# Feed-forward: the weight sums of every second unit made beside the input projection

## The chip, the cores and the metric

The kernel runs on one core of one Trainium2 chip. Its time is the device time of one execution in microseconds (us), of that core. Several executions are timed and the median is given; one execution more is recorded by the hardware profiler. The core has engines that each work through a queue of their own in a fixed order: PE (TensorE, matrix products), DVE (VectorE), ACT (ScalarE), POOL (GpSimd), and SP (SyncE), which in this kernel issues nearly all transfers (DMA) between the memory of the chip (DRAM) and the on-chip memory (SBUF).

## The reference

One layer of a hybrid trunk over 2048 tokens and 16 learned meta tokens, width 1024, all in float32:

```
p = rms_norm(h) @ w_in                      # input projection, 1024 x 3080
oa, ob, oc = rg_lru(p), forgetting_attention(p), rwkv7(p)
h = h + rms_norm(concat(oa, ob, oc) @ w_out)
f = causal_dwconv(rms_norm(h) @ ffn_up)     # 1024 x 5632, then 3 taps in time
gate, val = split(f)
h = h + rms_norm((gelu(gate) * val) @ ffn_down)
```

`rms_norm` divides a row by its root mean square and multiplies by a gain. The change concerns the weights `ffn_up` of the feed-forward part. They are inputs of the kernel and depend on nothing that is computed.

## The kernel before

**Stages.** The input projection runs in three parts of tokens (`for part in range(3)` in `hybrid_block_kernel`, L1978), each with 24 blocks of 128 output columns. Beside parts 1 and 2, and for some time behind them, the recurrences (RG-LRU and RWKV-7) of tokens that are already projected are worked off, a step or two at a time (class `Beside`). Then come attention, the output projection, the up projection of the feed-forward part (`ffn_up`, L1670) and the down projection (class `Down`).

**Precision.** Each operand of a matmul is kept as a high and a low part (`split`, L1574: ACT writes the high part, DVE or POOL the difference), and each product is three matmuls (`mm3`, L168 to L170).

**The up projection** works in three passes (`sup` 0, 1, 2) over blocks of tokens. In each pass it goes over 22 units `j`; a unit is a block of 128 gate columns and the 128 value columns that belong to it. A unit is computed by seven products in the manner of Strassen and Winograd instead of eight: three of them take quarters of the weights as they are (`g0`, `g1`, `v1`) and four take sums of the quarters `g0`, `v0`, `v1`, `g1` (`SUMS`, L1588):

```
s1 = v0 + v1,  s2 = s1 - g0,  s3 = g0 - v0,  s4 = g1 - s2
```

The products stand in `PRODUCTS` (L1524). The same sums serve all three passes. In pass 0 a unit is its "own" (`UpWeights`, L1615): the four raw quarters are loaded (256 KB each, L1634), POOL makes the four sums (L1648), and each sum is stored to DRAM (`scr["us"]`, L1649) as soon as it is made. In passes 1 and 2 all seven weights are loaded, the sums from `scr["us"]`. The weights of unit `j + 1` are prepared during the products of unit `j`. Of the seven low parts of a unit, POOL makes one in pass 0 (product 6) and two in passes 1 and 2 (products 3 and 6), by `POOLED`, L1659; DVE makes the others. Ten buffers (`uq`) hold raw weights and sums.

**Around it.** POOL also multiplies gate and value (`ending`, L1693) and makes sums of the token operands of the next pass (`ffn_sums`, L1570). DVE adds up products in PSUM (L1728, L1731, L1734), does two taps of the convolution (L1687), the low parts (L1576), and normalises the tokens of the next pass: `between` (L2069) calls `ffn_norm` (L1531) in even units, which loads 128 rows `xt` (L1536) and scales them on DVE (L1537).

**Sums of the down weights.** `weight_sums` (L1591) makes sums of the down projection's weights in the same way, ten units of one load of 1 MB, four POOL operations and one store of 1 MB, through a single buffer of four quarters (pool `us`). They are called for between the turns of the input projection (L2012: two of three turns of parts 1 and 2). A turn is one step of the generator `w_in_part` (25 in each of these parts: the gate columns, 22 column blocks, and the last two by token blocks).

**What sets the order.** The program is written in one order, but a planner with a model of the engines (`schedule_with_timeline_sim`, L2165) sets the order of each engine's queue: an instruction may be moved ahead of others when its inputs and its buffer are ready by the model. `tc.issue_after(x)` keeps instructions of the same engine behind `x`. On the chip each queue runs in that fixed order, and an instruction that waits holds those behind it.

**The projection's stores.** `w_in_step` (L203) computes a block of columns for a block of tokens, and SP stores it (L220, L221, L227). Columns of the values (`kind == "v"`) are transposed first and stored a step later (L241, L246).

Of the kernel before, what the change touches and what calls it, by code (L numbers as in the profile page):

```python
# [1 line left out]

# [6 lines left out]
F32 = mybir.dt.float32  # L9
# [4 lines left out]
ALU = mybir.AluOpType  # L14
# [4 lines left out]
P = 128  # L19
# [6 lines left out]
PAD = 64  # L26
A_ROWS = 512
C_ROWS = 1024
FF = 2816
NFF = FF // P  # L30
# [173 lines left out]
def w_in_step(core, pools, psum, weights, block, kind, c0, scr):  # L204

    nc = core.nc
    wh, wl = weights
    st = pools["st"]
    t0, n, tl, hi, lo = block
    ps = psum.tile([P, 512], F32, tag="mm", name=core.n("psp"))  # L210
    for k in range(KD):
        mm3(nc, ps[:, :n], wh[:, k], wl[:, k], hi[:, k], lo[:, k], k == 0, k == KD - 1)
    if kind in ("q", "k"):
        sc = 0.125 if kind == "q" else 1.0
        r0 = c0 - (512 if kind == "q" else 1024)
        oh = st.tile([P, 400], F32R, tag="sth", name=core.n("sth"))
        ol = st.tile([P, 400], F32R, tag="stl", name=core.n("stl"), bufs=1)
        nc.scalar.activation(oh[:, :n], ps[:, :n], AF.Copy, scale=sc)
        nc.vector.scalar_tensor_tensor(ol[:, :n], ps[:, :n], sc, oh[:, :n], op0=ALU.mult, op1=ALU.subtract)
        nc.sync.dma_start(scr[kind + "h"][r0 : r0 + P, t0 : t0 + n], oh[:, :n].bitcast(F32))  # L220
        nc.sync.dma_start(scr[kind + "l"][r0 : r0 + P, t0 : t0 + n], ol[:, :n].bitcast(F32))  # L221
        return
    o = st.tile([P, 400], F32, tag="sth", name=core.n("stp"))
    core.evac(o[:, :n], ps[:, :n])
    if kind != "v":
        r0 = c0 if kind == "a" else c0 - 2056 + A_ROWS
        nc.sync.dma_start(scr["p"][r0 : r0 + P, PAD + t0 : PAD + t0 + n], o[:, :n])  # L227
        return

    def turn():  # L230

        r0 = c0 - 1536
        pt = psum.tile([P, 4, P], F32, tag="mm", name=core.n("psv"))
        for i, (s, rows) in enumerate(tl):
            nc.tensor.transpose(pt[:rows, i], o[:, s - t0 : s - t0 + rows], core.ident[:])
        ot = st.tile([P, 4, P], F32, tag="stv", name=core.n("stv"), bufs=1)
        i0 = 0
        if tl[0][1] < P:
            s, rows = tl[0]
            core.evac(ot[:rows, 0], pt[:rows, 0])  # L240
            nc.sync.dma_start(scr["v"][s : s + rows, r0 : r0 + P], ot[:rows, 0])  # L241
            i0 = 1
        m = len(tl)
        core.evac(ot[:, i0:m], pt[:, i0:m])
        s = tl[i0][0]
        nc.sync.dma_start(  # L246
            scr["v"][s : s + P * (m - i0), r0 : r0 + P].rearrange("(j p) c -> p j c", p=P), ot[:, i0:m]
        )

    return turn  # L250
# [1334 lines left out]

SUMS = ("s2", "s4", "s3", "s1")  # L1588


def weight_sums(core, pool, w_down, scr):  # L1591

    nc = core.nc
    sub = lambda o, x, y: nc.gpsimd.tensor_tensor(o, x, y, op=ALU.subtract)
    for k in range(DOWN_PAIRS):
        t = pool.tile([P, 4, 512], F32, tag="us", name=core.n("ds"))
        nc.sync.dma_start(
            t[:].rearrange("p (i h) c -> p i (h c)", h=2),
            w_down[2 * P * k : 2 * P * (k + 1), :].rearrange("(i p) c -> p i c", p=P),
        )  # L1600
        l0, r0, l1, r1 = (t[:, i] for i in range(4))
        sub(l0, r0, l0)
        sub(r0, r1, r0)
        sub(r1, r1, l0)
        sub(l1, l1, r1)
        nc.sync.dma_start(scr["ds"][k], t[:].rearrange("p s c -> p (s c)"))
        yield
# [7 lines left out]
class UpWeights:  # L1615
# [2 lines left out]

    def __init__(self, core, raws, ring, w_up, scr, j, sup):
        self.core, self.raws, self.ring, self.w_up, self.scr, self.j = core, raws, ring, w_up, scr, j  # L1620
        self.own = sup == 0
        self.raw = {s: self.load(s) for s in ("g0", "v0", "v1", "g1")} if self.own else {}

    def new(self):
# [313 lines left out]
def hybrid_block_kernel(ctx: ExitStack, tc: tile.TileContext, args, out):  # L1938
    a = {s: v[0] if s != "meta_tokens" else v for s, v in args.items()}
    nc = tc.nc  # L1940
    core = Core(tc, ctx)
    scr = scratch(tc, ctx, core)
# [8 lines left out]
    def pool(es, name, bufs, **kw):  # L1951
        return es.enter_context(tc.tile_pool(name=name, bufs=bufs, **kw))
# [11 lines left out]
    with ExitStack() as p1:  # L1964
# [7 lines left out]
        with ExitStack() as p1a:  # L1972
            ps_mm = pool(p1a, "ps_mm", 5, space=PSUM)
            g_pre = spread(pool(p1a, "gpre", 1), a["norm_mix_pre"], "g_pre")
            pools = {"xn": pool(p1a, "xn", 1), "nt": pool(p1a, "nt", 4), "w": pool(p1a, "w", 2), "st": pool(p1a, "st", 2)}
            sums = weight_sums(core, pool(p1a, "us", 1), a["ffn_down"], scr)
            following = w_in_norm(core, pools, ps_mm, x, meta, g_pre, 0)
            for part in range(3):  # L1978
                blocks = following
# [28 lines left out]
                for i, _ in enumerate(units, READY + 1 if part == 0 else 1):  # L2008
                    if i == READY + 1:
                        beside.add(recurrences(core, R, lk, a["fox_f_bias"], scr, blocks, part))  # L2010
                    beside.advance()
                    if part and i % 3:  # L2012
                        next(sums, None)
                run(sums) if part == 2 else None
                if part < 2:
# [12 lines left out]
    with ExitStack() as p3:  # L2028
# [38 lines left out]
        sums, ws, down = [iter(())], [], []  # L2067
# [101 lines left out]
```

## Time and profile before

| | us |
|---|---|
| median of 3 runs | 3058.98 |
| lowest and highest of them | 3055.77, 3062.25 |
| the execution that was profiled, its time | 3059.87 |
| its span, from the first to the last instruction | 3058.1 |
| input projection parts 1 and 2 | about 330 to 845 |
| up projection, passes 0, 1 and 2 | from 1675, 2000 and 2295 to 2590 |

Times in the profile are microseconds from the start of the span. Rows of groups give line, engine, operation, tiles written and read, shapes and count, then after the bar the busy time, the mean of one in nanoseconds, and after the next bar the engine's idle time in front of them and what ended it. Rows of waits read "engine line waited for: total us, times, longest". Rows of the order of time give start, duration and the instruction, with the idle time in front of it in square brackets. PEclk is the share of the full TensorE clock that was granted. "SPq" is SP issuing a transfer; a transfer lands some time later.

### The profile page before, as it was taken

The page shows a single profiled execution, that of the slowest core. Times are in us where ns is not written, and L with a number is a line of the kernel's source. Part 1 is how long each engine was busy: PE and PEld are TensorE (multiplying, and loading weights), DVE is VectorE, ACT ScalarE, POOL GpSimd, SP SyncE. Part 2 cuts the span into 40 slices and gives each one's busy share as a digit, 9 for nine tenths or more (in the row PEclk, how much of TensorE's full clock was granted, in tenths as well). Part 3 has the DMA queues.
Part 4 walks back from the last instruction along what each step waited for, and adds up shares of the span by engine and source line. Part 5 has one row for each costly group of instructions (what it writes and reads, how often), then busy time and mean ns, then how long its engine had stood idle before and what let it go on. Part 6 is the DMA issues. An engine that isn't in the chain of part 4 may idle for free.

```text
span 3058.1 us, 52158 instructions
## 1 busy us (share of the span) xinstructions
PE 2876.4 (94%) x18488; PEld 2468.6 (81%) x18488; DVE 2162.6 (71%) x4232; ACT 1467.4 (48%) x2772; POOL 1312.2 (43%) x1436
## 2 busy tenths in 40 slices
PE   6998999999978999999988999999999999999998
PEld 6987998999855555664567999999999998787876
DVE  6247656676778888677556879887778787547766
ACT  4145344354545445445544545566566665324333
POOL 3310101001134557456723667833453334557765
PEclk8999999999968989999999999999999999999999
DMA  6664333353352346344264555565556565435444
GB/s 213 226 203 143 106 91 112 109 153 114 90 127 73 92 106 166 101 116 107 56 200 138 172 173 170 180 178 170 163 163 171 165 190 172 165 102 171 147 163 145
DMA packets 455477, 443.70 MB, mean 145 GB/s; under 512 B 81472, under 2 KB 372490, under 8 KB 452384
## 3 DMA queue, kind: packets, MB, share of 16 engines
q1 hardware_dynamic: 454832, 439.98, 48.6%
q8 instruction: 145, 2.38, 0.3%
q14 instruction: 116, 0.95, 0.1%
q0 software_dynamic: 384, 0.39, 0.0%
HBM read 314.39 MB, written 125.87 MB: 144 GB/s over the span
## 4 chain that ended last, share of the span: by engine, by line
PE 39%; DVE 7%; DMA 6%; POOL 5%; issue 3%; ACT 2%; SPq 0%; POOLq 0%; DVEq 0%; ACTq 0%
PE psu L168 8%; PE psu L169 7%; PE psu L170 7%; PE psd L170 2%; PE po L682 2%; PE psd L169 2%; PE psd L168 2%; DMA u<-scr_ff 2%; PE pswo L168 2%; PE pswo L170 2%; PE pswo L169 1%; PE mx L530 1%; DMA uq<-in_ffn_up_dram 1%; DVE uw L1576 1%; PE sc L659 1%
## 5 line engine op out<-in xcount | busy, mean ns | idle before, releaser
L168 PE MATMUL psu<-xo,uw 128*128 128x344 f32 x1848 | 592.5, 325 | 27.0 <-ACT xo L1575 7.7
L169 PE MATMUL psu<-xo,uw 128*128 128x344 f32 x1848 | 595.3, 322 | 0.0
L170 PE MATMUL psu<-xo,uw 128*128 128x344 f32 x1848 | 584.9, 321 | 0.0
L168 PE MATMUL psp<-xh,wh 128*128 128x384 f32 (+2 forms) x1152 | 381.0, 331 | 0.0
L170 PE MATMUL psp<-xh,wl 128*128 128x384 f32 (+2 forms) x1152 | 379.0, 329 | 0.0
L169 PE MATMUL psp<-xl,wh 128*128 128x384 f32 (+2 forms) x1152 | 377.5, 328 | 0.0
L168 PEld LDWEIGHTS psu<-xo,uw 128*128 128x128 f32 x1848 | 349.2, 190 | 31.3 <-ACT u L1726 8.2
L1576 DVE TENSOR_TENSOR uw<-uq,uw 128x512 fp32r<-128x512 f32 x352 | 331.4, 948 | 53.1 <-ACT uw L1575 50.9
L169 PEld LDWEIGHTS psu<-xo,uw 128*128 128x128 f32 x1848 | 350.4, 190 | 0.0
L170 PEld LDWEIGHTS psu<-xo,uw 128*128 128x128 f32 x1848 | 348.8, 190 | 0.0
L1575 ACT ACTIVATE uw<-uq 128x512 fp32r<-128x512 f32 x462 | 287.1, 627 | 93.0 <-PE psu L170 48.0
L664 ACT ACTIVATE p<-sc,bias 128x512 f32<-128x512 f32 (+4 forms) x352 | 197.2, 590 | 200.0 <-PE sc L660 165.3
L1687 DVE SCALAR_TENSOR_TENSOR uy<-psu,ffn_cols,uy 128x342 f32<-128x342 f32 (+1 forms) x396 | 223.7, 566 | 71.5 <-ACT uy L1685 70.3
L703 POOL TENSOR_TENSOR acc<-acc,p 128x512 f32<-128x512 f32 (+3 forms) x208 | 229.8, 1107 | 78.4 <-DVE acc L703 32.1
L1693 POOL TENSOR_TENSOR uy<-uy,uy 128x342 f32<-128x342 f32 (+1 forms) x132 | 146.7, 1111 | 218.8 <-DVE uy L1687 99.2
L1576 POOL TENSOR_TENSOR uw<-uq,uw 128x512 fp32r<-128x512 f32 x110 | 158.7, 1443 | 179.2 <-ACT uw L1575 149.9
L170 PEld LDWEIGHTS psp<-xh,wl 128*128 128x128 f32 x1152 | 220.3, 191 | 6.9 <-issue 5.6
L169 PEld LDWEIGHTS psp<-xl,wh 128*128 128x128 f32 x1152 | 220.2, 191 | 6.8 <-issue 5.4
L168 PEld LDWEIGHTS psp<-xh,wh 128*128 128x128 f32 x1152 | 220.3, 191 | 4.2 <-issue 1.9
L533 DVE TENSOR_REDUCE mc<-mx 128x1 f32<-128x400 f32 (+6 forms) x320 | 171.9, 554 | 49.2 <-PE mx L530 46.7
L1576 DVE TENSOR_TENSOR fo<-u,fo 128x896 fp32r<-128x896 f32 x88 | 108.5, 1233 | 122.0 <-ACT fo L1575 122.0
L1648 POOL TENSOR_TENSOR uq<-uq,uq 128x512 f32<-128x512 f32 x88 | 132.1, 1504 | 114.4 <-DMA uq<-in_ffn_up_dram 90.4
(460 smaller groups left out, 6393.3 us busy)
## 6 DMA issues: line engine op xcount, KB each, us to landing
uq<-in_ffn_up_dram SPq DMA_DIRECT2D x220, 256.0 KB
uq<-scr_us SPq DMA_DIRECT2D x176, 256.0 KB
raw<-in_w_in_dram SPq DMA_DIRECT2D x72, 512.0 KB
scr_us<-uq SPq DMA_DIRECT2D x88, 256.0 KB
u<-scr_ff SPq DMA_DIRECT2D x88, 256.0 KB
scr_ff<-uy SPq DMA_DIRECT2D x110, 171.0 KB
q<-scr_qh SPq DMA_DIRECT2D x96, 128.0 KB
ds<-in_ffn_down_dram SPq DMA_DIRECT2D x10, 1024.0 KB
```

What stands on the lines that cost most here:

```text
L168: nc.tensor.matmul(out, ah, bh, start=first, stop=False, skip_group_check=more)
L169: nc.tensor.matmul(out, ah, bl, start=False, stop=False, skip_group_check=more)
L170: nc.tensor.matmul(out, al, bh, start=False, stop=last, skip_group_check=more)
L533: self.reduced = nc.vector.tensor_reduce(mc[:rows, i, ci : ci + 1], ps[:rows, :full], axis=AX.X, op=ALU.max)
L664: last = nc.scalar.activation(p[:rows, :w], ps[:rows, :w], AF.Exp, bias=bias[:rows, j : j + 1])
L682: mm = nc.tensor.matmul(po[at : at + 64, c0:n], v1[:rows, j], p[:rows, : n - c0], start=start and i < 2, stop=end and i + 2 >= len(group), ...
L703: eng.tensor_tensor(a, ps_[0][0][:rows, c0:n] if start and i == 1 else a, p[:rows, : n - c0], op=ALU.add)
L1575: core.nc.scalar.activation(hi, src, AF.Copy)
L1576: (eng or core.nc.vector).tensor_tensor(lo, src, hi, op=ALU.subtract)
L1648: core.nc.gpsimd.tensor_tensor(raw[:], self.raw[x][:], self.raw[y][:], op=op)
L1687: stt(y[:, :n], src[:, i : n + i], cw[:, 44 * i + cc : 44 * i + cc + 1], y[:, :n], op0=ALU.mult, op1=ALU.add)
L1693: core.pooled = nc.gpsimd.tensor_tensor(v[:, :n], g[:, :n], v[:, :n], op=ALU.mult)
```

## The change

The sums of the even units `j` = 0, 2, ... 20 are no longer made in pass 0. A new generator `up_sums` makes them beside the input projection, called behind `weight_sums` in one chain and through the same single buffer: four loads of 256 KB, four POOL operations in place, and two turns later one store of 1 MB; after one turn more the next unit. Its loads and stores are kept behind the store that the input projection issued last in program order (`core.stored`, not renewed by the `v` columns). `SUMS` is reordered so that the four sums stand in `scr["us"]` as they stand in the buffer. The chain is called in every turn of parts 1 and 2, no longer in two of three. In pass 0 odd units stay their own; even ones load all seven weights, as in passes 1 and 2, and by `POOLED` give POOL two low parts.

```diff
-        nc.sync.dma_start(scr[kind + "l"][r0 : r0 + P, t0 : t0 + n], ol[:, :n].bitcast(F32))
+        core.stored = nc.sync.dma_start(scr[kind + "l"][r0 : r0 + P, t0 : t0 + n], ol[:, :n].bitcast(F32))
...
-        nc.sync.dma_start(scr["p"][r0 : r0 + P, PAD + t0 : PAD + t0 + n], o[:, :n])
+        core.stored = nc.sync.dma_start(scr["p"][r0 : r0 + P, PAD + t0 : PAD + t0 + n], o[:, :n])
...
-SUMS = ("s2", "s4", "s3", "s1")
+SUMS = ("s2", "s3", "s1", "s4")
+
+
+def up_sums(core, pool, w_up, scr, after):
+
+    nc = core.nc
+    tt = nc.gpsimd.tensor_tensor
+    for j in range(0, NFF, 2):
+        t = pool.tile([P, 4, 512], F32, tag="us", name=core.n("us"))
+        g0, v0, v1, g1 = (t[:, i] for i in range(4))
+        with after():
+            for o, r0, c0 in ((g0, 0, 0), (v0, 0, FF), (v1, 512, FF), (g1, 512, 0)):
+                nc.sync.dma_start(
+                    o.rearrange("p (k c) -> p k c", c=P),
+                    w_up[r0 : r0 + 512, c0 + P * j : c0 + P * j + P].rearrange("(k p) c -> p k c", p=P),
+                )
+        tt(v1, v0, v1, op=ALU.add)
+        tt(v0, g0, v0, op=ALU.subtract)
+        tt(g0, v1, g0, op=ALU.subtract)
+        tt(g1, g1, g0, op=ALU.subtract)
+        yield
+        yield
+        with after():
+            nc.sync.dma_start(scr["us"][j], t[:].rearrange("p s c -> p (s c)"))
+        yield
...
-        self.own = sup == 0
+        self.own = sup == 0 and j % 2 == 1
...
-            sums = weight_sums(core, pool(p1a, "us", 1), a["ffn_down"], scr)
+            kept = pool(p1a, "us", 1)
+            sums = chain(
+                weight_sums(core, kept, a["ffn_down"], scr),
+                up_sums(core, kept, a["ffn_up"], scr, lambda: tc.issue_after(core.stored.ins)),
+            )
...
-                    if part and i % 3:
+                    if part:
                         next(sums, None)
```

More of the change, by code (lines that the diff above doesn't have):

```diff
@@ L1 @@
+from itertools import chain
 from contextlib import ExitStack, nullcontext
```

## The prediction

> **What bounds the kernel now.** I read the page's summary first, then the busy time of each engine by stage, because the busy share of the span averages stages with different limits. The columns of the stage view are: stretch, its length, then busy time and instruction count of PE, PEld, DVE, ACT and POOL, granted clock, DMA share, GB/s.
>
> ```profile
> span 3058.1 us, 52158 instructions
> ...
> PE 2876.4 (94%) x18488; PEld 2468.6 (81%) x18488; DVE 2162.6 (71%) x4232; ACT 1467.4 (48%) x2772; POOL 1312.2 (43%) x1436
> ```
>
> ```profile
> 46.00:200.00 154.00, 146.81 (x804) 145.50 (x804) 48.77 (x63) 41.02 (x61) 54.42 (x37) 0.97 0.69 230
> 330.00:613.00 283.00, 279.84 (x2535) 257.12 (x2535) 175.52 (x405) 113.83 (x202) 26.25 (x54) 0.98 0.35 103
> 613.00:845.00 232.00, 228.08 (x2476) 208.18 (x2474) 169.58 (x392) 116.94 (x215) 22.66 (x42) 0.99 0.42 119
> 845.00:1000.00 155.00, 126.99 (x1198) 90.40 (x1198) 127.47 (x370) 73.37 (x160) 62.77 (x103) 0.77 0.43 102
> 1675.00:2000.00 325.00, 306.74 (x1884) 303.28 (x1885) 280.33 (x383) 181.77 (x362) 228.85 (x161) 0.97 0.54 171
> 2000.00:2295.00 295.00, 295.00 (x1880) 294.86 (x1881) 229.28 (x369) 186.21 (x367) 125.98 (x106) 1.00 0.59 169
> ```
>
> The last two rows are the first and the second pass (`sup` 0 and 1) over the 22 up-projection units: the same matmuls (1884 and 1880), yet 325 us against 295. The first pass is 30 us longer. PE is idle for 325 - 306.7 = 18.3 us of it, and its clock is 0.97 instead of 1.00, which is 0.03 x 325 = 9.8 us. The two make 28 of the 30.
>
> Next I asked who waits in the first pass, for SP, DVE and PE (total, times, longest):
>
> ```profile
> SPq L1649 <- POOL uq L1648: 144.4, 77, 5.8
> ...
> DVE xt L1537 <- DMA xt<-scr_h: 22.8, 5, 7.5
> DVE uy L1687 <- ACT uy L1685: 12.9, 23, 1.0
> DVE uw L1576 <- ACT uw L1575: 8.3, 12, 1.4
> ...
> PE psu L168 <- ACT u L1726: 7.6, 2, 5.5
> PE psu L168 <- DVE vb L1731: 5.0, 5, 2.9
> ```
>
> and in the second pass for DVE:
>
> ```profile
> DVE xt L1537 <- DMA xt<-scr_h: 3.2, 2, 1.6
> ```
>
> The SP queue spends 144.4 of 325 us waiting to store weight sums that POOL has not finished; the `xt` loads of `ffn_norm` stand in that queue. DVE, which is in order, stands 22.8 us at `xt`, against 3.2 in the second pass. One of these stalls in order of time, on SP, DVE and PE:
>
> ```profile
> 1725.51 0.32 SPq L1649 DMA_DIRECT2D scr_us<-uq  x1
> 1726.85 0.32 SPq L1694 DMA_DIRECT2D scr_ff<-uy  x1
> 1727.26 3.52 SPq L1634 DMA_DIRECT2D uq<-in_ffn_up_dram  x3
> 1730.87 0.46 SPq L1536 DMA_DIRECT2D xt<-scr_h  x1
> ...
> 1735.69 1.44 DVE L1537 SCALAR_TENSOR_TENSOR xt<-xt,rsv,g_fpre 128x1024 f32<-128x1024 f32 x1 [5.34 <-DMA xt<-scr_h]
> ...
> 1745.85 0.65 PE L168 MATMUL psu<-xo,uw 128*128 128x344 f32 x1 [2.95 <-DVE vb L1731]
> ...
> 1745.10:1751.90 6.80, 6.05 (x21) 6.05 (x22) 5.81 (x12) 4.51 (x11) 2.29 (x2) 0.50 0.55 158
> ```
>
> DVE waits 5.34 us, works its backlog off without a pause, drains a PSUM bank late, and PE stands 2.95 us; then the clock is 0.50 for 6.8 us, another 3.4 us. So the first pass is bound by DVE with its waits: 280.3 busy + 22.8 + 12.9 + 8.3 = 324.3 of 325. POOL makes DVE slower too (columns: count, busy us, mean ns; first pass, then second):
>
> ```profile
> L1576 DVE TENSOR_TENSOR uw<-uq,uw 128x512 fp32r<-128x512 f32 x129 | 138.6, 1085 | 8.4 <-ACT uw L1575 8.3
> L1687 DVE SCALAR_TENSOR_TENSOR uy<-psu,ffn_cols,uy 128x342 f32<-128x342 f32 x126 | 71.0, 565 | 13.0 <-ACT uy L1685 12.5
> L1687 DVE SCALAR_TENSOR_TENSOR uy<-vb,ffn_cols,uy 128x342 f32<-128x342 f32 x42 | 35.7, 849 | 0.4 <-ACT uy L1685 0.4
> ...
> L1576 DVE TENSOR_TENSOR uw<-uq,uw 128x512 fp32r<-128x512 f32 x110 | 94.8, 865 | 22.4 <-ACT uw L1575 21.9
> L1687 DVE SCALAR_TENSOR_TENSOR uy<-psu,ffn_cols,uy 128x342 f32<-128x342 f32 x132 | 74.8, 568 | 27.2 <-ACT uy L1685 26.9
> L1687 DVE SCALAR_TENSOR_TENSOR uy<-vb,ffn_cols,uy 128x342 f32<-128x342 f32 x44 | 25.0, 568 | 0.0
> ```
>
> With POOL busy 229 us instead of 126, the operations with both tensors in SBUF (`uw`, `uy<-vb`) take 1085 and 849 ns instead of 865 and 568; the one that reads PSUM does not change (565, 568).
>
> **The change part by part.** *Removed from the first pass.* Eleven units (even `j`) lose 4 sums on POOL and 4 stores on SP, load 3 transfers more, and by `POOLED` move one more low-part split from DVE to POOL, as all units of the second pass do.
>
> ```profile
> L1648 POOL TENSOR_TENSOR uq<-uq,uq 128x512 f32<-128x512 f32 x80 | 120.9, 1512 | 83.5 <-DMA uq<-in_ffn_up_dram 65.9 <-DVE uw L1576 14.3 <-POOL uq L1648 0.7
> ...
> L1576 POOL TENSOR_TENSOR uw<-uq,uw 128x512 fp32r<-128x512 f32 x23 | 35.5, 1543 | 2.2 <-DMA uq<-scr_us 1.2 <-ACT uw L1575 1.0
> ```
>
> POOL: about half of 80 sums, 40 x 1.512 = -60.5 us, and 11 x 1.543 = +17 us; 229 becomes 185 us. DVE: halfway between the two passes, (280.3 + 229.3)/2 = 255 us. SP: half of the 144.4 us, 72, and the stores that go are those in front of `xt`: `xt` is loaded in even units, and the stores just ahead of it belong to the operands of that even unit, made in the odd one before. With `xt` waits even at half of 22.8 DVE needs 255 + 11 + 21 = 287 us, under the 295 of PE: the bound moves back to PE.
>
> What can be won is 30 us less what the start of the stage costs (its clock is 0.50 for the first 5.2 us, 2.6 us):
>
> ```profile
> 1675.00:1680.20 5.20, 4.66 (x16) 4.66 (x17) 5.20 (x4) 2.83 (x7) 3.02 (x2) 0.50 0.27 101
> ```
>
> so at most -27 us. If stalls simply follow the number of units with sums, half, -13.5; if each remaining unit still jams, a third, -9. Since DVE's total falls below PE's I take -20, nearer to the row of the second pass, and leave 7 us for bursts in odd units.
>
> *Added beside the input projection* (parts 1 and 2, 330 to 845 us): 44 loads of 256 KB and 11 stores of 1 MB on SP, 44 sums on POOL, one `us` buffer. The nearest rows are the ten `weight_sums` units, which the planner has pulled up to 26 to 193 us, with the waits there:
>
> ```profile
> L1594 POOL TENSOR_TENSOR ds<-ds x40: 1261/1298/2246, 32.3 to 190.3; 128x512 f32<-128x512 f32 x40
> L1597 SPq DMA_DIRECT2D ds<-in_ffn_down_dram x10: 368/383/415, 26.4 to 179.0; - x10
> ...
> SPq L1606 <- POOL ds L1594: 31.0, 8, 6.8
> SPq L1597 <- DMA scr_ds<-ds: 18.2, 8, 3.8
> ...
> PE eps L408 <- DVE ccol L400: 7.2, 2, 6.9
> ```
>
> Issuing: 55 x 0.383 = 21 us of SP over 515 us, a queue that mostly waits there for data. POOL: 44 x 1.298 = 57 us on an engine busy 26 + 23 of 515 us. DMA: 22 MB more at shares of 0.35 and 0.42; at 0.69, in 46 to 200 us, PE lost nothing to transfers: its only wait of size, 7.2 us, is another chain. That covers the traffic at nothing; without PE's five PSUM banks it would be the late stores' waits of a few us each.
>
> The new waits: a load waits for the landing of the store before it, a store for the sums. Behind them on SP stand the projection's stores, the next weights and the recurrences' transfers. In the rows above these two cost (31.0 + 18.2)/8 = 6 us a unit, in a cycle of (179.0 - 26.4)/9 = 17 us. Here the store is queued two turns behind the load and the next load one turn on; a part has 25 turns, so a turn is 283/25 = 11 us and 232/25 = 9 us, a cycle 28 to 34 us, more than 17: the waits should end before SP comes to them. Only in the four `v` turns, which do not renew `core.stored`, do they stand close, perhaps 6 us twice a part, within PE's PSUM banks.
>
> What is not covered is the recurrences: PE meets them with little to spare, and their solving alternates POOL and DVE.
>
> ```profile
> L1134 POOL TENSOR_TENSOR rwitmp<-rwix,rwia x75: 236/409/1357, 358.3 to 798.3; 128x16 f32<-128x16 f32 x5, 128x24 f32<-128x24 f32 x5, 128x32 f32<-128x32 f32 x5, 128x40 f32<-128x40 f32 x5
> L1135 DVE TENSOR_REDUCE rwix<-rwitmp x75: 164/221/288, 359.4 to 799.8; 128x8 f32<-128x16 f32 x5, 128x8 f32<-128x24 f32 x5, 128x8 f32<-128x32 f32 x5, 128x8 f32<-128x40 f32 x5
> ...
> PE rps L1158 <- DVE rwxu L1174: 1.5, 1, 1.5
> ```
>
> A batch of four sums holds POOL 5.2 us. The five solving chains take 15 steps each, about 15 x (0.41 + 0.22) = 9.5 us without their gaps, say 13. An estimate: a batch meets one with (13 + 5.2) x 5/515 = 18%, 2 of 11, each up to 5.2 us: 10 us. Operations of DVE in SBUF slowed by sums add at most some 57 us x (849/568 - 1) = 28 us of DVE time, of which a third may lie on PE's path: 9. Bounds 0 (as at 46 to 200 us) and +19; the planner knows of the sums and fills PE with projection matmuls, so I take +3.
>
> *Start of the up projection, order of the four sums.* Unit 0 now loads its sums; the stage starts on the token operands, not on weights. The new order only names other quarters of a tile: 0.
>
> Sum, against the execution profiled: 3059.87 (span 3058.1) - 20 + 3 = 3042.9. It lies 0.9 above the median 3058.98, so 3042.
>
> Two sentences from the Trainium skill, which the sum does without. "GPSIMD Engine Reference", Key points, says that POOL shares its SBUF interfaces with VectorE and contends with DVE instructions of two SBUF inputs; the trace agrees (849 against 568, and 565 against 568 with PSUM), and by it the moved sums take DVE time again in the projection, the second rival below. "TensorE: Matmul & The Clock Gate", Part 1, has the clock fall after an idle window of about 3.4 us; the trace shows it at 0.50 behind an idle of only 2.95 us, and by the page that stall would cost 2.95 instead of 6.3 us; the measurement decides.
>
> **The rivals.** *The first pass comes down to the second altogether:* -27 + 3, 3035. For it: DVE's 287 of 295. Against: odd units still hold SP.
>
> *The `xt` stalls stay.* `xt` is loaded in even units, and these make the sums of the next odd unit: loads still meet stores at POOL's pace. Then only the shorter DVE operations help, -5, and with +3 the time is 3057: no change. For it: `xt` took 4.8 us from issue (1730.87 to 1735.69) even when nothing held it; against: the 3.2 us of the second pass.
>
> *Slower: sums in front of the recurrences.* POOL is in order; when loads land later than the planner thought, four sums stand in front of `rwitmp`, and PE, with projection matmuls planned behind the late recurrence matmul, stands. A stall of 5.2 us costs about 5.2 + 3.4 (the half clock above) = 8.6 us. With four of eleven batches it is 34, against -20: +14, 3073. It decides from three (26 us). Against: my estimate is two, and the waits of PE in 330 to 845 us are 1.5 us at most.
>
> *The change does not do what it says:* sums not done by 845 us, run on in the stretch to 1000 us where DVE (127 of 155 us) is full: some +5, 3064. The 10 + 33 turns fit into 50, so I hardly believe it.
>
> **How the numbers follow.** A run of this kernel tells about 0.2% (6 us) from no change. Forecast 3042: 0.48; full gain 3035: 0.17; stalls stay 3057: 0.18; slower 3073: 0.14; not done 3064: 0.03 (slower or same). Faster 0.48 + 0.17 = 0.65, same 0.19, slower 0.16. The forecast's own range is 3034 to 3052. From 3028 (27 won, a few us more from the planner's order) to 3062 leaves the slower cases out, about 0.2.
>
> **What would show it.** Right: the first pass at about 302 us, 44 `us` sums between 330 and 845 us, SP's wait for sums near 72 us, `xt` waits under 11 us, clock 0.99. In the projection, PE waits of no more than some 5 us added. Wrong: `xt` waits near 20 us, or matmuls of `rps` waiting over 3 us with POOL's sums ahead, or the stretch from 845 to 1000 us longer than 155 us.

## The result and the profile after

| | before | after |
|---|---|---|
| median, runs taken together (6 each), us | 3057.38 | 3079.99 |
| lowest and highest, us | 3048.93, 3066.00 | 3072.51, 3085.47 |
| execution profiled: time, span, us | 3059.87, 3058.1 | 3072.51, 3069.4 |

The changed kernel is slower: ratio 1.0069, 95% interval 1.0051 to 1.0087, or 22.6 us by the medians. The forecast of 3042 and its range up to 3062 are both missed. The execution of after that was profiled is the fastest of its six, so its trace holds only 11.3 us of span of the 22.6.

I cut both spans at the same pieces of work: from the same input-projection matmul (the 1857th record of `psp`; the sums of two of the eleven units run before it, from 440 us, those of nine behind it) to the last one, which I call the projection stretch; from there to the last attention matmul, the attention stretch; then passes 0 and 1. Rows are: from and to, length, busy us of PE, PEld, DVE, ACT and POOL with their counts, PEclk, DMA share, GB/s. Before:

```profile
495.50:844.00 348.50, 343.45 (x3489) 314.32 (x3488) 247.74 (x585) 166.33 (x306) 30.92 (x61) 0.99 0.40 114
844.00:1542.00 698.00, 634.81 (x3948) 396.67 (x3947) 526.93 (x1388) 337.89 (x647) 395.00 (x500) 0.91 0.41 103
1675.40:2000.20 324.80, 306.94 (x1885) 303.48 (x1886) 280.13 (x383) 181.57 (x363) 228.45 (x161) 0.97 0.54 171
```

and after:

```profile
491.40:869.30 377.90, 360.08 (x3524) 326.62 (x3523) 263.63 (x591) 166.64 (x308) 87.40 (x97) 0.95 0.54 159
869.30:1574.70 705.40, 637.38 (x3948) 398.52 (x3947) 523.84 (x1386) 335.35 (x647) 389.02 (x499) 0.90 0.41 102
1709.20:2010.40 301.20, 298.70 (x1880) 297.97 (x1881) 246.99 (x373) 185.02 (x362) 172.80 (x131) 0.99 0.57 175
2010.40:2306.20 295.80, 295.80 (x1888) 295.66 (x1886) 229.22 (x370) 186.70 (x367) 126.00 (x106) 1.00 0.59 168
```

Pass 0 gains 23.6 us (324.8 to 301.2), the projection stretch loses 29.4 (348.5 to 377.9), the attention stretch 7.4; the rest of the span is 1.9 shorter. Sum: +11.3, the difference of the spans. In the projection stretch PE stands 377.9 - 360.1 = 17.8 us instead of 5.0, and its clock is 0.955 instead of 0.985 (rounded in the rows): 0.045 x 377.9 = 17 us lost to half clock instead of 5. The two make some 25 of the 29.4.

Pass 0 went as the first part of the prediction had it. Waits and groups of after, 1709 to 2010 us:

```profile
SPq L1674 <- POOL uq L1673: 67.9, 40, 4.7
...
DVE xt L1538 <- DMA xt<-scr_h: 18.3, 5, 4.7
DVE uy L1712 <- ACT uy L1710: 17.9, 23, 1.8
DVE uw L1577 <- ACT uw L1576: 9.9, 15, 1.2
...
PE psu L169 <- ACT u L1751: 2.4, 2, 2.1
...
L1577 DVE TENSOR_TENSOR uw<-uq,uw 128x512 fp32r<-128x512 f32 x119 | 110.4, 936 | 10.6 <-ACT uw L1576 9.9
...
L1712 DVE SCALAR_TENSOR_TENSOR uy<-vb,ffn_cols,uy 128x342 f32<-128x342 f32 x42 | 30.1, 716 | 1.2 <-ACT uy L1710 1.1
```

SP's wait for sums halves (144.4 to 67.9), DVE's two SBUF groups become shorter (1085 to 936 ns, 849 to 716). The `xt` waits hardly shrink (22.8 to 18.3), but DVE, with less to do, takes them: PE's largest wait is 2.4 us in total where there were 7.6 and 5.0.

In the projection stretch PE waited for this before (the longest waits, of 5.1 us in all):

```profile
PE rps L1158 <- DVE rwxu L1174: 1.5, 1, 1.5
PE eps L408 <- DVE ccol L404: 1.5, 1, 1.5
```

and for this after (of 17.9 us in all):

```profile
PE eps L1021 <- ACT rwe L1022: 4.8, 2, 2.7
PE rps L1159 <- DVE rwxu L1175: 3.6, 2, 2.8
PE rps L1159 <- POOL rwitmp L1135: 2.6, 2, 1.9
PE rps L1311 <- DVE rww L1319: 2.2, 1, 2.2
```

Those of after are recurrence matmuls. Only 2.6 us of it end with a POOL operation; the rest waits for ACT or DVE. One such wait in order of time (start, duration, instruction; POOL, DVE, ACT, PE, then the row of the stretch behind it):

```profile
643.12 1.28 POOL L1605 TENSOR_TENSOR us<-us 128x512 f32<-128x512 f32 x1 [14.61 <-DMA us<-in_ffn_up_dram]
644.48 1.27 POOL L1606 TENSOR_TENSOR us<-us 128x512 f32<-128x512 f32 x1
645.72 0.79 POOL L1017 TENSOR_SCALAR rwe<-rwe 128x512 f32<-128x512 f32 x1
646.48 1.45 POOL L1607 TENSOR_TENSOR us<-us 128x512 f32<-128x512 f32 x1
648.01 2.07 POOL L1608 TENSOR_TENSOR us<-us 128x512 f32<-128x512 f32 x1
...
646.71 2.31 DVE L1034 TENSOR_TENSOR_SCAN rwe<-rst,rwe 128x512 f32<-128x512 f32 x1
648.94 2.22 DVE L164 TENSOR_TENSOR wl<-raw,wh 128x1024 fp32r<-128x1024 f32 x1
...
649.05 0.63 ACT L1039 ACTIVATE rwe<-rwe 128x512 f32<-128x512 f32 x1 [1.73 <-DVE rwe L1034]
649.59 0.46 ACT L1022 ACTIVATE rwe<-eps,rwkv_om 128x256 f32<-128x256 f32 x1
...
650.10 0.70 PE L1021 MATMUL eps<-rwwa,wa_up 64*128 64x256 f32 x2 [2.07 <-ACT rwe L1022]
...
651.80:658.60 6.80, 6.74 (x50) 4.90 (x49) 5.75 (x19) 3.72 (x9) 0.00 (x0) 0.50 0.50 135
```

The four sums run from 643 to 650 us; between them stands L1017, an operation of the recurrences that writes the scan's input. Beside the sums DVE's scan takes 2.31 us and a weight's low part 2.22 (means before: 1.21 and 1.22, below). ACT waits 1.73 us for the scan, PE 2.07 us for ACT, and then the clock is 0.50 for 6.8 us, another 3.4. The stall was 2 us, its price 5.5. Two causes are possible here: L1017 stands behind two sums in POOL's queue, and the scan is slow. The memset kernel below separates them.

### The profile page after: what moved, and what is told of

Same layout as the page of the kernel before. It is cut to its first block, busy times and chain, and to the rows that moved or that the text cites. A ratio compares the mean times of both kernels' runs of the same rounds, so it can differ in the third digit from the quotient of the medians.

```text
span 3069.4 us, 52209 instructions
## 1 busy us (share of the span) xinstructions
PE 2886.3 (94%) x18488; PEld 2474.5 (81%) x18488; DVE 2140.0 (70%) x4221; ACT 1468.3 (48%) x2772; POOL 1312.9 (43%) x1447
## 5 line engine op out<-in xcount | busy, mean ns | idle before, releaser
L170 PEld LDWEIGHTS psu<-xo,uw 128*128 128x128 f32 x1848 | 348.5, 189 | 0.0
L1577 DVE TENSOR_TENSOR uw<-uq,uw 128x512 fp32r<-128x512 f32 x341 | 301.0, 888 | 55.5 <-ACT uw L1576 52.3
L1577 POOL TENSOR_TENSOR uw<-uq,uw 128x512 fp32r<-128x512 f32 x121 | 173.2, 1432 | 220.1 <-ACT uw L1576 188.5
L1718 POOL TENSOR_TENSOR uy<-uy,uy 128x342 f32<-128x342 f32 (+1 forms) x132 | 138.7, 1051 | 285.4 <-DVE uy L1712 131.3
L1576 ACT ACTIVATE fo<-u 128x896 fp32r<-128x896 f32 x88 | 81.1, 922 | 205.9 <-POOL u L1828 115.9
```

What stands on the lines that cost most here:

```text
L170: nc.tensor.matmul(out, ah, bl, start=False, stop=False, skip_group_check=more)
L1576: core.nc.scalar.activation(hi, src, AF.Copy)
L1577: (eng or core.nc.vector).tensor_tensor(lo, src, hi, op=ALU.subtract)
L1718: core.pooled = nc.gpsimd.tensor_tensor(v[:, :n], g[:, :n], v[:, :n], op=ALU.mult)
```

## The experiments

Medians and ratios are against the runs of the kernel before on the same chip. The stretches are read as above, from each kernel's one profiled execution; one profile of one order is not exact: with all queues up to there the same, before, "pass 0 side alone" and the late scaling (the last group of experiments) have 345.5 to 351.6 us of projection and 697.5 to 706.3 of attention; after, "projection side alone" and "memsets" have 705.4 to 714.8 of attention.

| kernel | median us | ratio, 95% | projection | attention | pass 0 |
|---|---|---|---|---|---|
| before | 3057 to 3060 | 1 | 348.5 | 698.0 | 324.8 |
| after | 3079.99 | 1.0069, 1.0051 to 1.0087 | 377.9 | 705.4 | 301.2 |
| pass 0 side alone | 3037.71 | 0.9924, 0.9909 to 0.9939 | 345.5 | 697.5 | 305.8 |
| projection side alone | 3096.65 | 1.0119, 1.0101 to 1.0136 | 381.7 | 714.8 | 319.2 |
| no sums | 3057.62 | 0.9988, 0.9973 to 1.0003 | 363.5 | 698.8 | 301.5 |
| loads only | 3054.31 | 0.9984, 0.9965 to 1.0003 | 349.1 | 707.0 | 305.1 |
| sums, small transfers | 3069.43 | 1.0041, 1.0025 to 1.0056 | 362.2 | 711.7 | 301.8 |
| sums gated | 3084.91 | 1.0073, 1.0057 to 1.0089 | 368.0 | 722.5 | 301.0 |
| memsets for sums | 3069.72 | 1.0035, 1.0019 to 1.0050 | 367.0 | 711.2 | 301.4 |
| sums doubled | 3081.26 | 1.0063, 1.0039 to 1.0087 | 387.4 | 694.9 | 300.7 |
| before, pace 1.44 | 3082.18 | 1.0075, 1.0051 to 1.0099 | 342.3 | 720.6 | 323.4 |
| before, pace 1.52 | 3082.42 | 1.0073, 1.0055 to 1.0092 | 349.1 | 716.1 | 325.9 |
| after, pace 1.55 | 3060.04 | 0.9999, 0.9985 to 1.0013 | 374.3 | 692.5 | 304.3 |
| after, pace 1.60 | 3058.43 | 0.9999, 0.9985 to 1.0013 | 378.8 | 689.5 | 307.3 |

**The two sides apart.** *Pass 0 side alone*: the projection as before; the even units load raw quarters in the place of their sums, in all passes, so their sums are left out of the computation.

```diff
-        if s in SUMS:
+        if s in SUMS and j % 2 == 0:
+            r0, c0 = 512 * (SUMS.index(s) % 2), FF * (SUMS.index(s) // 2) + P * j
+            src = self.w_up[r0 : r0 + 512, c0 : c0 + P].rearrange("(k p) c -> p k c", p=P)
+        elif s in SUMS:
...
-                up_sums(core, kept, a["ffn_up"], scr, lambda: tc.issue_after(core.stored.ins)),
...
-                    if part:
+                    if part and i % 3:
```

> The pass 0 side alone: nothing is added to the projection; even units load raw quarters in place of their sums in all passes (so these sums are left out of the computation). If pass 0 gains by itself, it takes about 301 us and the kernel about 3057 - 24 = 3033 us. If the shorter pass 0 came with the shifted start, it takes 310 us or more and the gain is under 15 us.

*Projection side alone*: `up_sums` as in after, pass 0 as before, every unit its own.

```diff
-        self.own = sup == 0 and j % 2 == 1
+        self.own = sup == 0
```

> The projection side of the change alone: up_sums runs as in the changed kernel, but in pass 0 all 22 units make their sums as before. If costs and gain are separate, the whole cost shows: the projection ends near 869 us, pass 0 takes 325 us, in all about 3080 + 24 = 3104 us. If the loss was instead an accident of the order planned behind the projection, the time differs from that by more than 10 us.

The gain is real: 3037.7, some 21 to 23 us under before, where I had forecast 20. The loss is real too: the projection side alone costs 36 us. They don't simply add: on top of the projection side, the pass 0 side is worth 15 to 17 us (ratios 1.0119 and 1.0069, medians 3096.65 and 3079.99; pass 0 took 319.2 us without it and 301.2 with it). The loss had to be taken apart.

**What of the projection side costs.** *No sums*: the four POOL operations are taken out, the transfers stay; what is stored as sums are the raw quarters, so the sums of the even units are left out.

```diff
-        tt(v1, v0, v1, op=ALU.add)
-        tt(v0, g0, v0, op=ALU.subtract)
-        tt(g0, v1, g0, op=ALU.subtract)
-        tt(g1, g1, g0, op=ALU.subtract)
```

> The changed kernel without the 44 POOL sums beside the projection: its 44 loads and 11 stores stay, the even units get raw quarters as sums (so this part of the computation is left out). Theory A, the sums stand on POOL in front of the recurrences: the projection ends near 844 us again instead of 869, PE waits there fall from 18 to about 5 us, pass 0 stays at 301 us, in all about 3035 us, 0.7% under the kernel before. Theory B, the added transfers make the recurrences' and the projection's own transfers late: PE waits and the projection's end stay as in the changed kernel, about 3078 us.

*Small transfers*: the sums stay, on a buffer that is set once, but each transfer moves 8 KB; the even units load raw quarters in all passes, so their sums are left out.

```diff
-                    o.rearrange("p (k c) -> p k c", c=P),
-                    w_up[r0 : r0 + 512, c0 + P * j : c0 + P * j + P].rearrange("(k p) c -> p k c", p=P),
+                    o[:, 0:16],
+                    w_up[r0 : r0 + P, c0 + P * j : c0 + P * j + 16],
...
-            nc.sync.dma_start(scr["us"][j], t[:].rearrange("p s c -> p (s c)"))
+            nc.sync.dma_start(scr["us"][j, :, 0:16], t[:, 0, 0:16])
```

> The sums without the traffic: beside the projection the 44 sums and the 55 transfers are issued at the same places, but each transfer is cut to 8 KB (16 columns of 128 rows; the sums are then of mostly zeros). In pass 0 even units load raw quarters as in e4_pass0_alone (3037.7), so these sums are left out of the computation. If traffic and sums each cost about half, as 3057.6 of e1_no_sums against 3037.7 and 3080 suggests, this comes to about 3055 to 3060 us. If the sums only cost because POOL stands waiting for large loads, it comes to 3040 to 3045 us.

*Loads only*: "no sums" without the 1 MB stores; even units load raw quarters in all passes, the sums are left out.

```diff
-        with after():
-            nc.sync.dma_start(scr["us"][j], t[:].rearrange("p s c -> p (s c)"))
```

> The transfers without sums, and of these only the loads: the 1 MB stores are left out, and the even units load raw quarters in every pass, so the sums are left out of the computation. Against the pass 0 side alone (3037.7) and the loads and stores without sums (3057.6): if the stores are what delays the recurrences' small loads, 3037 to 3045; if the loads do, 3050 to 3058; if both share it, about 3047.

Projection rows of these three, in this order:

```profile
493.30:856.80 363.50, 352.65 (x3524) 320.66 (x3522) 248.97 (x586) 166.67 (x308) 30.68 (x61) 0.98 0.55 166
```

```profile
494.50:856.70 362.20, 347.64 (x3488) 316.62 (x3487) 265.06 (x577) 166.60 (x306) 81.76 (x97) 0.98 0.40 111
```

```profile
497.20:846.30 349.10, 343.59 (x3489) 313.35 (x3488) 246.32 (x587) 165.63 (x306) 30.24 (x60) 0.99 0.50 141
```

Transfers without sums lengthen the stretch by 15 us, sums without transfers by 14, together 29. The loads alone cost nothing that can be seen (349.1), so the stores should be the part of the traffic that costs; but the planner ordered these kernels differently, and with the same work in five orders (the runs of before and its variants below) the stretch was 342 to 357 us. That the stores cost is therefore likely, not shown. By its total the third kernel says the opposite (3054, which was expected if the loads cost). But of the 14.1 us by which its span exceeds that of "pass 0 side alone" (3052.9, 3038.8), 3.6 lie in the projection stretch and 9.5 in the attention stretch, where no such load runs any more. The totals of this group can't be split without the stretches.

**How the sums cost.** *Sums gated*: a DVE copy of one column, kept behind a later eviction of the projection, releases the sums, so that POOL does not stand waiting for loads with the recurrences behind it.

```diff
+        yield
+        with behind():
+            nc.vector.tensor_copy(v1[:, 0:1], v1[:, 0:1])
         tt(v1, v0, v1, op=ALU.add)
...
-        yield
```

> The changed kernel with one operation more: a copy of one column on DVE, queued behind an eviction of the next turn of the projection, releases each unit's sums, so that POOL gets them a turn after their loads were issued and never stands waiting for a load with recurrence work behind it. Theory A1, POOL's wait for the loads is the cost: PE waits in the projection fall to some 8 us, about 3045 us. Theory A2, the 5 us that four sums hold POOL are the cost, loads or not: little is won, about 3070 us. Theory B, the transfers: 3078 us.

*Memsets*: each sum is replaced by a POOL memset of 128x1400; it only writes. The sums are left out.

```diff
-        tt(v1, v0, v1, op=ALU.add)
...
+        for i in (0, 100, 200, 300):
+            nc.gpsimd.memset(t[:].rearrange("p s c -> p (s c)")[:, i : i + 1400], 0.0)
```

> The changed kernel with each sum replaced by a POOL memset of 128x1400, estimated at 1.3 us like the sum: POOL is occupied for about as long in the same places and after the same loads, but reads nothing. The sums are left out, so what pass 0 multiplies for the even units is not the reference's. If the sums cost by slowing VectorE through their reads, VectorE's busy time in the projection's window falls back to about 249 us and the time to that of the transfers alone, 3055 to 3062. If POOL's occupation costs, the time stays at 3073 to 3085 whatever VectorE's busy time is.

*Sums doubled*: ahead of each unit's four sums go four more like them, into a spare tile.

```diff
+        x = core.spare[:]
+        for a_, b_, op in ((v0, v1, ALU.add), (g0, v0, ALU.subtract), (v1, g0, ALU.subtract), (g1, v0, ALU.subtract)):
+            tt(x, a_, b_, op=op)
         tt(v1, v0, v1, op=ALU.add)
```

> The changed kernel with the POOL work of its sums doubled: each unit's four sums are preceded by four like them into a spare tile, 44 more operations of some 1.3 us. If what the sums cost is that VectorE is slowed while POOL reads SBUF beside it, VectorE's busy time between the first input projection matmul and the last (265 us with the sums, 249 without) grows by about as much again, to some 280 us, and the time by as much as the sums cost in the changed kernel beyond the transfers, 20 to 30 us: 3100 to 3110. If the cost is the transfers and the place in POOL's queue alone, VectorE stays near 265 and the time within 3075 to 3090.

The memset kernel is the cleanest of all: by the traces the queues of PE and of POOL are the same, instruction for instruction, as in after (with a memset in the place of each sum), and up to the end of attention as in "projection side alone". Its memsets take 1.27 us, as the first sums in the example above do (the sums take 1.49 on average, as they lengthen too), and they stand behind the same loads:

```profile
495.50:862.50 367.00, 354.11 (x3524) 322.15 (x3523) 250.85 (x590) 166.68 (x308) 77.54 (x97) 0.97 0.55 164
...
L1606 POOL MEMSET us<- 128x1400 f32 x36 | 45.7, 1270 | 130.7 <-DMA us<-in_ffn_up_dram 129.4
...
L1034 DVE TENSOR_TENSOR_SCAN rwe<-rst,rwe 128x512 f32<-128x512 f32 x4 | 4.9, 1215 | 0.0
```

DVE is busy 250.9 us, against 263.6 with sums. The same groups before:

```profile
L163 DVE TENSOR_TENSOR wl<-raw,wh 128x1024 fp32r<-128x1024 f32 x32 | 39.0, 1220 | 5.4 <-ACT wh L162 5.3
...
L1033 DVE TENSOR_TENSOR_SCAN rwe<-rst,rwe 128x512 f32<-128x512 f32 x4 | 4.9, 1213 | 0.1
...
L986 DVE SCALAR_TENSOR_TENSOR rwr<-rwraw,rwkv_cols,rwr 128x256 f32<-128x256 f32 x8 | 3.7, 480 | 1.7 <-ACT rwr L985 1.7
```

and after:

```profile
L164 DVE TENSOR_TENSOR wl<-raw,wh 128x1024 fp32r<-128x1024 f32 x32 | 41.5, 1298 | 8.8 <-ACT wh L163 7.4 <-PE eps L1015 1.3
...
L1034 DVE TENSOR_TENSOR_SCAN rwe<-rst,rwe 128x512 f32<-128x512 f32 x4 | 7.6, 1909 | 0.5 <-POOL rwe L1017 0.5
...
L987 DVE SCALAR_TENSOR_TENSOR rwr<-rwraw,rwkv_cols,rwr 128x256 f32<-128x256 f32 x8 | 5.6, 706 | 4.6 <-ACT rwr L986 4.6
```

The scan goes from 1213 to 1909 ns and `rwr` from 480 to 706; with memsets the scan stays at 1215. The place of the example above, in the memset kernel:

```profile
643.07 2.60 POOL L1606 MEMSET us<- 128x1400 f32 x2 [13.99 <-DMA us<-in_ffn_up_dram]
645.64 0.62 POOL L1017 TENSOR_SCALAR rwe<-rwe 128x512 f32<-128x512 f32 x1
646.20 2.59 POOL L1606 MEMSET us<- 128x1400 f32 x2
...
646.45 1.21 DVE L1034 TENSOR_TENSOR_SCAN rwe<-rst,rwe 128x512 f32<-128x512 f32 x1
647.59 1.19 DVE L164 TENSOR_TENSOR wl<-raw,wh 128x1024 fp32r<-128x1024 f32 x1
...
648.75 0.70 PE L1021 MATMUL eps<-rwwa,wa_up 64*128 64x256 f32 x2 [0.15 <-ACT rwe L1022]
...
651.80:658.60 6.80, 6.53 (x52) 5.82 (x51) 5.05 (x14) 3.81 (x8) 0.00 (x0) 1.00 0.34 85
```

L1017 comes as late as with sums (645.64 and 645.72 us), behind two memsets. But the scan takes 1.21 us and not 2.31, PE waits 0.15 us and not 2.07, and the clock stays at 1.00. So this stall comes from the slow scan and not from the place in POOL's queue.

With the sums doubled DVE is busy 281.8 us, and the stretch grows again:

```profile
494.40:881.80 387.40, 362.06 (x3523) 325.75 (x3522) 281.83 (x587) 166.53 (x309) 141.52 (x135) 0.95 0.52 156
881.80:1576.70 694.90, 634.48 (x3947) 397.15 (x3947) 520.10 (x1389) 337.33 (x647) 388.97 (x500) 0.92 0.42 104
```

So what the sums' reading of SBUF beside DVE costs is 377.9 - 367.0 = 11 us of the stretch, and 10 by the medians (3079.99, 3069.72), in the same order of the queues; "projection side alone", of the same order too, has 381.7 us, 15 more than with memsets. Some 13 us of DVE time (263.6 - 250.9) became 11 us of the time: the slowed scan stands in the chain that PE waits for in the example; that the other slowed operations do so elsewhere is likely, but not shown one by one. The Trainium skill says as much, "SBUF — State Buffer", section "Who interferes with whom": a DVE instruction with two SBUF inputs contends with a GpSimd instruction that reads SBUF, not with one that only writes it; 263.6, 281.8 and 250.9 us agree. What POOL's occupation costs beyond the transfers, 367.0 against 363.5, is within the scatter of orders, so it stays open. The total of the memset kernel, 3069.7, lies between its two expectations: the rest of its projection stretch (367.0 us, where before has 348.5) and the order of after remain.

The total of the doubled kernel stayed where after is, though its projection stretch is 9.5 us longer, and the gated kernel, whose stretch is 10 us shorter, was no faster. In both the attention stretch went the other way: 694.9 and 722.5 us. By 870 us nothing of the change runs. So there was a second cost, which none of these edits controls; it also leaves open whether the gate's 10 us come from the gate or from the order.

**The order.** The planner orders the queues by its model of the times; with work added in the projection it orders all that follows differently. PE's queue of the attention stretch is one and the same in before and "pass 0 side alone" (698.0, 697.5 us), and another one in after, "projection side alone" and "memsets" (705.4, 714.8, 711.2). That hints at the order, though three kernels further down have the order of before and 696.6, 696.7 and 706.3. To test the order alone I changed only the pace at which the recurrences are written into the program: no work is added or removed.

```diff
-PACE = 1.5
+PACE = 1.44
```

> The kernel before with the pace of the recurrences in the program's order 1.44 steps a turn in place of 1.5. No work is added or taken away; only the order in which the planner queues it changes, and 154 matmuls of the recurrences stand behind the last input projection matmul, in place of 150 (158 in the changed kernel). If the order is a cost of its own, and that of the kernel before a favourable one, 3064 to 3075, with the stretch from the last projection matmul to the last of the attention at 705 to 715 us in place of 698. If the order costs nothing, 3055 to 3061.

> The kernel before with 1.52 steps a turn: 151 matmuls of the recurrences behind the last projection matmul, again no work added. If any other order than that of the kernel before costs, 3062 to 3072; if only the number of recurrence matmuls left behind counts, 3057 to 3061; if the order costs nothing, 3055 to 3061.

and in the changed kernel 1.55 and 1.60:

> The changed kernel with 1.55 steps a turn, by which 147 recurrence matmuls are left behind the last projection matmul in place of 158. If the longer attention stretch of the changed kernel (705 us, 711 and 715 in two others of the same order) comes from its order, this one has it at 695 to 702 and takes 3067 to 3073, unless the projection's own order gets worse. If the stretch is longer for another reason, it stays at 705 or more and the time at 3077 to 3084.

> The changed kernel with 1.6 steps a turn, 146 recurrence matmuls left. As with 1.55: 3067 to 3075 if the order is what the attention stretch pays for, 3077 to 3084 if not. Together with 1.55 it shows how far the time scatters over orders of the same work; in no order does the projection's stretch return to 348 us if sums and transfers cost by themselves.

The kernel before loses 23 us by a pace of 1.44 and as much by 1.52, more than any of the theories expected. The changed kernel wins 20 us by 1.55 and by 1.60, and is then as fast as before. Rows of before at 1.44 and of after at 1.60:

```profile
492.80:835.10 342.30, 339.31 (x3487) 310.00 (x3485) 242.46 (x565) 165.91 (x306) 30.95 (x60) 1.00 0.41 116
835.10:1555.70 720.60, 646.50 (x3947) 403.13 (x3947) 532.84 (x1408) 336.39 (x647) 387.65 (x500) 0.90 0.40 100
```

```profile
492.10:870.90 378.80, 361.00 (x3533) 327.52 (x3531) 274.11 (x593) 167.34 (x309) 87.61 (x97) 0.95 0.54 159
870.90:1560.40 689.50, 629.25 (x3939) 391.67 (x3937) 522.54 (x1384) 337.42 (x646) 395.26 (x500) 0.92 0.42 105
```

The attention stretch runs from 689 to 722 us over orders of the same work, more than the 10 us by which one order scatters. The difference is nearly all stalls and their half clock: 720.6 - 646.5 = 74 us idle and 0.10 x 720.6 = 72 lost to the clock in the one, 60 and 53 (clock 0.923) in the other; without them they are 575 and 576. The projection stretch of the changed kernel stays at 374 to 379 in three orders (381.7 in "projection side alone"), that of the kernel before at 342 to 357 in five. So the added work lengthens the projection stretch in every order tried, and the attention stretch goes with the order.

**Is a faster pace better as such?** Asked on the kernel before with another edit, which the profile of pass 0 suggested: the scaling of `xt` is kept behind the convolution tap that DVE does last before it, so that DVE does not stand at `xt` with work behind it.

```diff
-    nc.vector.scalar_tensor_tensor(xt[:rows], xt[:rows], rs[:rows], gain[:rows], op0=ALU.mult, op1=ALU.mult)
+    with core.tc.issue_after(core.swept.ins) if hasattr(core, "swept") else nullcontext():
+        nc.vector.scalar_tensor_tensor(xt[:rows], xt[:rows], rs[:rows], gain[:rows], op0=ALU.mult, op1=ALU.mult)
...
-            stt(y[:, :n], src[:, i : n + i], cw[:, 44 * i + cc : 44 * i + cc + 1], y[:, :n], op0=ALU.mult, op1=ALU.add)
+            core.swept = stt(y[:, :n], src[:, i : n + i], cw[:, 44 * i + cc : 44 * i + cc + 1], y[:, :n], op0=ALU.mult, op1=ALU.add)
```

> The kernel before with one thing changed: in ffn_norm the scaling of xt on DVE is queued behind the last tap of the unit before, so that the planner cannot put it ahead of its place in the program, where the load has not landed. If the 22.8 us that DVE stands at xt in pass 0 are what binds pass 0, pass 0 falls from 325 to about 305 us and the kernel to about 3040 us, with all sums still made in pass 0. If SP's wait for the sums or POOL's load on DVE binds it, pass 0 stays over 318 us.

At the pace of before it takes 3047.79 us, ratio 0.9957 (0.9941 to 0.9973): faster than both kernels, with PE's queue of before up to the end of attention. Pass 0 takes 308.5 us and no `xt` wait is left in it; its execution profiled was the slowest of its runs, with 706.3 us of attention in the order of before, which shows how far one profile can be off. With three units of the change on top (`for j in 4, 8, 12`, their transfers not kept behind the projection's stores, each store right behind its sums), the time is the same, 3047.18 (0.9961, 0.9942 to 0.9980); these three units without the late scaling give 3056.68 (0.9996, 0.9982 to 1.0011), not the 3050 expected. There pass 0 gains 6.4 us (318.4), but the stretch from the first projection matmul to the first of part 1, in which the three units' sums now run (204 to 247 us), takes 274.8 us in the place of 267.0 (277.3 together with the late scaling): 2.6 us a unit, about as much as the 29.4 us for eleven.

> v1_scaled_later and v3_three_units together. If both work on the same stalls of DVE at xt, it gains little over the better of the two (3 us); if one works on xt and the other on POOL's load, the gains add.

> Sums of three units alone (4, 8 and 12) beside the projection, not queued behind its stores, so that the planner puts them right behind the sums of the down weights at about 193 to 245 us, mostly ahead of the recurrences. If the recurrences are what suffers, the projection costs under 5 us, pass 0 gains in proportion to its units, 3 of 11, or more as these are units with an xt load: 6 to 12 us, in all about 3050 us. If traffic costs wherever it is put, the projection's end moves by 5 us or more and nothing is won.

Then the late scaling with a pace of 1.55 and 1.60:

> The kernel before with the late scaling of pass 0 (3047.8 at a pace of 1.5) and a pace of 1.55: 141 recurrence matmuls behind the last projection matmul. If a faster pace shortens the attention stretch as it did in the changed kernel (692 us), this takes 3038 to 3043, the best of all. If the orders only scatter, anything from 3040 to 3072, with an attention stretch of 690 to 722.

> The same with 1.6 steps a turn, 149 recurrence matmuls left. If the pace is what shortens the attention stretch, 690 us and 3036 to 3043; if the number of recurrence matmuls left counts, 697 us and 3045 to 3050; if the orders only scatter, 3040 to 3072.

1.55 gives 3066.01 us (1.0015, 1.0003 to 1.0027), with 356.6 us of projection and 709.2 of attention; 1.60 gives 3043.50 (0.9954, 0.9938 to 0.9971), with 349.8 and 699.0, the same as 1.5 by the ratios. So a faster pace is not better as such, nor is it the number of recurrence matmuls left behind the projection that counts: before and its slower variants at 1.44 and 1.52 have the same number in the traces (1666), the late scaling 1634 at 1.55 and 1664 at 1.60. The orders scatter.

## Why the prediction was wrong

By the spans the sum of -17 became +11.3, 28.3 us off: the projection 26.4 (29.4 for 3), the attention stretch 7.4 (for nothing), pass 0 3.6 better than forecast, the rest 1.9. The median of after lies 7.5 us above its profiled execution; no trace shows where.

**Pass 0: right, in size too.** Forecast 302 us, clock 0.99, SP waiting 72 us for sums; measured 301.2, 0.99 and 67.9. Alone it is worth 21 to 23 us, forecast 20. One reason in it failed: the `xt` waits were to be under 11 us and are 18.3. DVE still fits beside PE, as it has 33 us less to do (280.1 to 247.0): 247.0 + 18.3 + 17.9 + 9.9 = 293 of 301.2 us, with less room than the 287 that I had counted. That this is why PE hardly waits is argued; no run separates it. The late scaling shows what the `xt` waits were worth by themselves: without them, and with all sums still made there, pass 0 takes 308.5 us, 16 less.

**"That covers the traffic at nothing": not borne out, not settled.** The 44 loads fit (349.1 us). With the eleven 1 MB stores the stretch is 363.5, above all orders of the same work without them (342 to 357). The row I leaned on, 46 to 200 us at a DMA share of 0.69, has hardly any recurrence matmuls: it could show that projection weights stand the traffic, not that small loads of a dependent chain do.

**"+3" for the recurrences, the step that failed: mis-sized, and by the wrong mechanism.** I let DVE's slow-down count for at most 28 us, a third of it on the path, then took 3 since the planner would fill PE. It measured 13 to 16 us of DVE time (263.6 to 265.1 us against 249.0 and 250.9 without reads) and 11 to 15 us of the time: about as much, not a third. The half clock behind each stall, which I priced in the rival (5.2 + 3.4), was left out of the bounds of this term, and it is nearly half of the loss: 12.8 us more idle, some 12 more at half clock. That the planner would fill PE with projection matmuls, my reason for +3 instead of more, did not hold: no more than some 5 us of PE waits added was to be the sign of it, and it is these 12.8. Together the projection costs 29, above my bound of 19; of that the reads are 11 to 15, and the rest (transfers, POOL's occupation) is not split.

**"A few us more from the planner's order": the term that was missing.** I gave the order of the queues a few us in the range and no term. It is worth 23 us in the kernel before with no other change, and 20 in the changed one. With the pace at 1.55 or 1.60 the changed kernel is at 3058 to 3060: there pass 0 and a shorter attention stretch pay for the projection.

**The rivals.** "Slower: sums in front of the recurrences" forecast 3073, nearest to the result, by another mechanism: sums in front of `rwitmp` in POOL's queue. PE's waits ended by `rwitmp` are 2.6 us, and memsets in the same places give a stretch 3.5 us longer than the transfers alone, in another order; that some of it comes from POOL's queue is not excluded. What I kept as a cost of a third on the path, DVE's slow-down, is the mechanism that the runs show. "The change does not do what it says" is out: the last sum starts at 797.6 us. My sign for wrong, the stretch from 845 to 1000 us growing, pointed at the right place for a wrong reason.

## What to carry to other kernels

Where a planner orders the queues by a model, a change in one stage reorders the ones behind it. Before a change is blamed or praised, run it in two or three orders of the same work, and read each stage for itself. Work moved to an engine with time to spare is not free if its reads slow the operations of a chain on which another engine waits; a short stall of PE is to be priced with the half clock behind it.

## What the runs showed of the hardware

- A POOL operation of 1.3 us that reads SBUF lengthens DVE's operations with two SBUF inputs (scan 1213 to 1909 ns mean, 2.31 us in the example); a memset of the same length does not (1215 ns, and 1.21 us at the same place). An operation with one of its inputs in PSUM did not change (`rwsc<-rps,rmask`, 679 to 682 ns).
- The clock fell to 0.50 for 6.8 us behind a PE wait of 2.07 us, and stayed at 1.00 in the memset kernel, where the same matmul waited 0.15 us. The Trainium skill, "TensorE: Matmul & The Clock Gate", Part 1, puts the fall behind an idle window of about 3.4 us. No such window was idle throughout here, and the measurement decides: stalls well below that length cost the clock too.
